# Moving four operand splits of a down projection ahead of the last instructions of the up projection in two engine queues

## The chip, the core and the metric

The kernel runs on one core of one Trainium2 chip. Its engines work side by side, each through a queue of its own in order: TensorE (matrix products, PE in the profile), VectorE (DVE), ScalarE (ACT), GpSimd (POOL) and SyncE (SP), which issues most of the DMA transfers. An instruction that waits holds up everything queued behind it on its engine. The metric is the time of one execution on the device, in microseconds (us); lower is better.

## What is computed

One layer of an encoder for 2304 positions (2048 of one request, 256 of another): a mixer (mLSTM heads and attention heads), and then the feed-forward part, which is where the change lies:

```python
    h = rmsnorm(x, norm2_w)
    u = centred_dwconv(h @ w_up, conv_w, conv_b)
    a, g = jnp.split(u, 2, axis=-1)
    return x + (jax.nn.silu(g) * a) @ w_down
```

`w_up` is 1024 x 5632, `w_down` 2816 x 1024, all in 32-bit floats. The convolution runs over positions with three taps: the centre one and two neighbours.

## The kernel before

**Products in halves.** Each operand of a large product is split in two tiles: a high part, made by a copy to a type with fewer bits on ScalarE, and a low part, the difference of the source and the high part, made on VectorE. A product is then three TensorE instructions: high x high, high x low, low x high. Both operands of a group must be split before its three products are complete. In the down pass this is `halves` (L1395 to L1398): L1397 on ScalarE, L1398 on VectorE.

**Seven products for eight.** The up pass and the down pass each multiply 2 x 2 blocks with seven block products and additions, under the names 11, 21, t2, t1, t3, 22, t4. In the up pass `up_start` (L1204) and its inner `rest` do this for a pair of channel chunks: the products accumulate in three PSUM tiles p1, p2, p3, ScalarE copies them out (`copy`, L1244) and VectorE adds (`add`, L1247). The last three steps of `rest` are the product 22, the add into `u12`, the product t4, and the copy into `u21`. `u12` belongs to the first chunk of the pair, `u21` to the second.

**The up pass** (`phase_u`, L1267) goes over two blocks of positions, and in each over 11 groups of two chunks. A group does `up` for its gate half, a SiLU (L1352), `up` for its other half, and the product of both (L1355). After each `up` comes `conv` (L1323) for both chunks: the centre tap on ScalarE (L1329, which writes `y`), a small copy (L1334), two neighbour taps on VectorE (L1336), and two corrections of one column on ScalarE (L1340) at the border of the two requests. There are three `y` buffers. GpSimd stores the results in tiles `a_d` in DRAM, with four sums and differences of them (L1357 to L1366).

**The down pass** (`phase_e`, L1369) goes over the seven block products, in each over three column groups z, and in each over 11 weight tiles p. For one p it issues 12 products (L1555): four output groups m of three products. Output groups 0 and 1 go to one PSUM tile, 2 and 3 to the next one of four tiles used in turn with the up pass; the second tile is the one that held p1 of the last `up`, which that `up`'s last copy empties. Each p needs one weight tile `we` (raw load `dw`, L1431, four raw buffers; 13 split buffers), and each four p one activation tile `te` (load L1440, four buffers, split in place). `fetch_w(WA)` and `fetch_t(2)` (L1514, L1515) ask for the first two of each ahead of the loop; later ones are asked for within it, the third weight tile during p = 0.

**Memory.** The pools of the down pass lie on the stack where those of the up pass lay: `e_t` (te) from the base, over the operands in `d_1`, then `e_w` (we) and `e_r` (dw). A tile waits only for those older tiles that it overlaps. An operand tile of the up pass takes 18,560 bytes of a partition, a `te` 12,288, a `we` 4,096.

**Order.** The order of instructions on each engine isn't that of the program text. A planner at build time replays the program with modelled durations and lets each engine take the instruction that is ready, the earlier one in the text first. A manual dependency between two instructions of one engine adds no wait on the chip; it only tells the planner which comes first.

Of the kernel before, what the change touches and what calls it, by code (L numbers as in the profile page):

```python
# [11 lines left out]
AF = mybir.ActivationFunctionType  # L12
ALU = mybir.AluOpType
# [22 lines left out]
BLK = 1152  # L36
# [56 lines left out]
def f32(ap):  # L93
    return ap.bitcast(F32)


class Ctx:
    pass


def rstd_of(g, pool, ms, n, name):
# [1038 lines left out]
def n2_ops(pool, b, which):  # L1140

    return {k: pool.tile([P, NCC // 2, 2, NH], F32R, tag="n" + k, name=f"n{k}_{b}", bufs=1) for k in which}
# [61 lines left out]
def up_start(g, s1, bank, ops, b, jj, rs=None):  # L1204


    nc = g.nc
    n = (DT[b + 1] - DT[b]) // 2
    m = n // 2
    nm = f"{b}_{jj}"  # L1210
    r1, r2 = rs or up_load(g, s1, b, jj)
    h = D // 2
    a11, a12, a21, a22 = r1[:, 0:h], r1[:, h:D], r2[:, 0:h], r2[:, h:D]
    t1, t2, t4 = (s1[0].tile([P, h], F32, tag="tmp", name=f"tw{k}_{nm}", bufs=3) for k in (1, 2, 4))

    def mul(p, k, src, add=False):

        i = g.nwu = (g.nwu + 1) % WU
        w = s1[i // 3].tile([P, 2, NCC // 2, P], F32R, tag="wu", name=f"wu{k}_{nm}", bufs=3 if i < 3 else WU - 3)
        hi, lo = (w[:, a].rearrange("p c n -> p (c n)") for a in range(2))  # L1220
        nc.scalar.activation(hi, src, AF.Copy)
        nc.vector.tensor_tensor(lo, src, f32(hi), ALU.subtract)
        for z in range(2):
            for c in range(NCC // 2):
                for i, (aa, bb) in enumerate(((0, 0), (0, 1), (1, 0))):
                    nc.tensor.matmul(p[:, z], w[:, aa, c, :], ops[k][:, c, bb, z * m:z * m + m],  # L1226
                                     start=c == 0 and i == 0 and not add, stop=c == NCC // 2 - 1 and i == 2,
                                     skip_group_check=add)
    p1, p2 = bank("a" + nm)[:, :, 0:m], bank("b" + nm)[:, :, 0:m]
    mul(p1, "11", a11)  # L1230
    mul(p2, "21", a12)

    nc.gpsimd.tensor_tensor(t1, a21, a22, ALU.add)
    nc.gpsimd.tensor_tensor(t2, t1, a11, ALU.subtract)
    nc.gpsimd.tensor_tensor(a21, a11, a21, ALU.subtract)
    nc.gpsimd.tensor_tensor(t4, a12, t2, ALU.subtract)

    def rest(u1, u2):


        u11, u12, u21, u22 = (u[:, k * n:k * n + n].rearrange("p (z t) -> p z t", z=2) for u in (u1, u2) for k in range(2))

        def copy(o, p):
            nc.scalar.activation(o, p, AF.Copy)  # L1244

        def add(o, p, q):
            nc.vector.tensor_tensor(o, p, q, ALU.add)  # L1247
        copy(u11, p1)
        add(u11, p2, u11)
        mul(p1, "t2", t2, True)  # L1250
        copy(u12, p1)
        p3 = bank("c" + nm)[:, :, 0:m]
        mul(p3, "t1", t1)
        copy(u21, p3)
        mul(p1, "t3", a21, True)
        add(u22, p1, u21)
        mul(p3, "22", t4, True)
        add(u12, p3, u12)
        mul(p1, "t4", a22, True)
        copy(u21, p1)  # L1260
    return rest


# [3 lines left out]
def phase_u(g, tc, s1, pd, ops, first):  # L1267


    nc = g.nc  # L1270
    ND = T // BLK
    groups = [list(range(j, j + 2)) for j in range(0, NFC, 2)]
    with ExitStack() as st:
# [14 lines left out]
        cw = cp.tile([P, 4, 2 * NFC], F32, name="cw")  # L1288
        NC = NW - BLK
        carry = cp.tile([P, 2 * NFC, NC], F32, name="carry")  # L1290
        sl = st.enter_context(tc.tile_pool(name="d_l", bufs=1, reuse_waits="tile"))
        late = n2_ops(sl, 0, ("t4", "22"))
        su = st.enter_context(tc.tile_pool(name="d_u", bufs=1, reuse_waits="tile"))
        for k in range(UB):
# [11 lines left out]
        for b in range(ND):  # L1306
            nn = DT[b + 1] - DT[b]
            if b:
                ops = n2_ops(s1[0], b, EARLY)
                ops.update(n2_ops(sl, b, ("t4", "22")))  # L1310
                ops.update(n2_ops(sl2, b, ("t3", "t1")))
                for k, e in zip(OPS, P1):
                    n2_load(g, ops, b, k, engs=e)

            def up(j):

                rest = first.pop(0) if first else up_start(g, s1, bank, ops, b, j)
                us = [su.tile([P, NW], F32, tag="u", name=f"u{b}_{j + k}", bufs=UB) for k in range(2)]
                o = NC if b else 1
                rest(*(u[:, o:o + nn] for u in us))  # L1320
                return [conv(j + k, u) for k, u in enumerate(us)]

            def conv(jj, u):  # L1323
                if b:
                    nc.scalar.activation(u[:, 0:NC], carry[:, jj, :], AF.Copy)
                if b < ND - 1:
                    nc.scalar.activation(carry[:, jj, :], u[:, BLK:NW], AF.Copy)
                y = sa.tile([P, BLK], F32, tag="y", name=f"y{b}_{jj}", bufs=YB)
                nc.scalar.activation(y, u[:, 1:1 + BLK], AF.Identity, scale=cw[:, 1, jj:jj + 1], bias=cw[:, 3, jj:jj + 1])  # L1329
                cut = T1 - b * BLK  # L1330
                if cut < BLK:

                    yc = sp.tile([P, 2], F32, tag="yc", name=f"yc{b}_{jj}", bufs=2)
                    nc.scalar.activation(yc, y[:, cut - 1:cut + 1], AF.Copy)  # L1334
                for k, (s, e) in ((0, (0 if b else 1, BLK)), (2, (0, BLK if b < ND - 1 else BLK - 1))):
                    nc.vector.scalar_tensor_tensor(y[:, s:e], u[:, s + k:e + k], cw[:, k, jj:jj + 1], y[:, s:e],  # L1336
                                                   ALU.mult, ALU.add)
                if cut < BLK:
                    for t, k in ((cut - 1, 0), (cut, 2)):
                        nc.scalar.activation(y[:, t:t + 1], u[:, t + k:t + k + 1], AF.Identity,  # L1340
                                             scale=cw[:, k, jj:jj + 1], bias=yc[:, t - cut + 1:t - cut + 2])
                return y

            def store(k, gi, t):
                nc.gpsimd.dma_start(g.a_d[gi // TG][DOPS.index(k), :, gi % TG, b * HB:(b + 1) * HB], t)

            for gi, gr in enumerate(groups):
                if b < ND - 1 and SG <= gi < SG + NCC // 2:
                    n2_sums(g, sa, b + 1, gi - SG)
                ygs = up(gr[0] + NFC)  # L1350
                for y in ygs:
                    nc.scalar.activation(y, y, AF.Silu)  # L1352
                yas = up(gr[0])
                for y, yg in zip(yas, ygs):
                    nc.vector.tensor_tensor(y, y, yg, ALU.mult)  # L1355
                b11, b12, b21, b22 = (y[:, k * HB:(k + 1) * HB] for y in yas for k in range(2))
                t1, t2, t4 = (sa.tile([P, NH], F32, tag="tc", name=f"tc{k}_{b}_{gi}", bufs=3)[:, 0:HB] for k in (1, 2, 4))  # L1357
                store("11", gi, b11)
                nc.gpsimd.tensor_tensor(t1, b12, b11, ALU.subtract)
                nc.gpsimd.tensor_tensor(t2, b22, t1, ALU.subtract)  # L1360
                for k, t in (("t2", t2), ("21", b21), ("t1", t1)):
                    store(k, gi, t)
                nc.gpsimd.tensor_tensor(b12, b22, b12, ALU.subtract)
                nc.gpsimd.tensor_tensor(t4, b21, t2, ALU.subtract)
                for k, t in (("t3", b12), ("22", b22), ("t4", t4)):
                    store(k, gi, t)  # L1366


def phase_e(g, tc, pd):  # L1369


    nc = g.nc
    h = D // 2
    G3 = TW // CG
    with ExitStack() as st:
# [16 lines left out]
            sy.tile([P, 4], F32, tag="rcol", name=f"place_rcol{k}", bufs=2)  # L1392
        swb = st.enter_context(tc.tile_pool(name="e_v", bufs=1, reuse_waits="tile"))

        def halves(t, src):  # L1395
            lo, hi = t[:, 1], t[:, 0]
            nc.scalar.activation(hi, src, AF.Copy)  # L1397
            nc.vector.tensor_tensor(lo, src, f32(hi), ALU.subtract)  # L1398

        def down(f, o, p):  # L1400
            return g.w_down[0, (2 * p + f) * P:(2 * p + f + 1) * P, o * h:o * h + h]
# [101 lines left out]
        def fetch_w(n):  # L1503
            while wq and n > 0:
                k = wq.pop(0)
                ws[k] = weight(*k)
                n -= 1

        def fetch_t(n):
            while tq and n > 0:  # L1510
                k = tq.pop(0)
                ts[k] = acts(*k)
                n -= 1
        fetch_w(WA)  # L1514
        fetch_t(2)  # L1515
        todo = {}
        SZ = NP * G3

# [11 lines left out]
        for z in range(G3):  # L1530
            e = 2 * SZ + z * NP
            at(e + 3, lambda z=z: resid(0, 0, z))
            at(e + 8, lambda z=z: collect(0, z, squares(0, 0, z)))
            e = 4 * SZ + (z + 1) * NP
# [4 lines left out]
            e = 5 * SZ + (z + 1) * NP  # L1539
            at(e + 2, lambda z=z: resid(1, 1, z))  # L1540
            at(e + 8, lambda z=z: collect(1, z, squares(1, 1, z)))
            e = 6 * SZ + (z + 1) * NP
# [3 lines left out]
        for i, k in enumerate(DOPS):  # L1546
            for z in range(G3):
# [21 lines left out]
                if end:  # L1569
                    fetch_t(1)  # L1570
                    qs = []
                    for m in range(2):
# [5 lines left out]
                        q = squares(0, 1, z, (2 * m, 2 * m + 1))  # L1578
# [224 lines left out]
```

## Time and profile before

| | |
|---|---|
| median of three runs | 3371.0 us (3368.56 to 3371.91) |
| span of the profiled execution, first to last instruction | 3372.4 us |
| TensorE busy in the span | 3271.5 us |
| last product of the up pass ends | 2850.21 us after the span's start |
| first product of the down pass starts | 2857.31 us |
| mean granted TensorE clock over the span | 0.986 |

The page gives a span, and no time of its own, for the profiled execution. A row of a timeline gives start, length (both in us), engine, line, operation, output and inputs, their shapes, the number of instructions, and in brackets how long the engine was idle before it and which instruction ended that. In names, numbers are left out: `te` stands for all activation tiles. L1226 are the products of the up pass, L1555 those of the down pass. A chain of waits goes back from the last instruction to whatever released each step. PEclk is the share of TensorE's clock that was granted; 0.50 means that products take twice as long.

### The profile page before, as it was taken

What the parts mean: (1) busy time and instruction counts of PE and PEld (TensorE: products, weight loads), DVE (VectorE), ACT (ScalarE), POOL (GpSimd) and SP (SyncE); (2) the same over time, 40 slices, a digit from 0 to 9 for tenths busy, and PEclk for the clock granted to TensorE, in tenths of its full rate; (3) what the DMA queues carried; (4) which work ended last, traced back from release to release, by engine and by line L of the source; (5) the groups of instructions that cost most, each with busy time, mean ns of one, the idle gap of its engine ahead of it and who ended that gap; (6) DMA issues with size and microseconds to landing.
All of it is one profiled execution on the core that took longest, in us unless ns stands there. A gap on an engine that the chain in (4) does not pass through costs nothing. (4 is left out here: it accounts for less than half of the span.)

```text
span 3372.4 us, 57131 instructions
## 1 busy us (share of the span) xinstructions
PE 3271.5 (97%) x21366; PEld 3047.6 (90%) x21366; DVE 2403.1 (71%) x3727; ACT 1802.4 (53%) x3781; POOL 1327.6 (39%) x1686
## 2 busy tenths in 40 slices
PE   8899999999999999899999999999999999999998
PEld 6788888888888888788889999999999998999998
DVE  7875687777768788876766778877877776544573
ACT  5545666667666777665552544445555555323331
POOL 8652133213333323211246457645554442851112
PEclk9999999999999999999999999999999999999999
DMA  8765343343336444433347334424322223885563
GB/s 273 229 201 150 94 126 97 105 125 98 113 108 188 130 135 128 123 99 96 103 133 263 129 102 148 127 96 176 107 93 97 100 93 102 302 274 172 164 223 107
DMA packets 300636, 483.03 MB, mean 143 GB/s; under 512 B 36597, under 2 KB 186279, under 8 KB 300359
## 3 DMA queue, kind: packets, MB, share of 16 engines
q1 hardware_dynamic: 247543, 348.34, 32.8%
q0 software_dynamic: 36256, 121.60, 10.8%
q10 hardware_dynamic: 16560, 9.44, 0.9%
q8 instruction: 168, 2.75, 0.3%
q14 instruction: 109, 0.89, 0.1%
HBM read 337.37 MB, written 141.91 MB: 142 GB/s over the span
## 5 line engine op out<-in xcount | busy, mean ns | idle before, releaser
L622 DVE TENSOR_TENSOR pl<-ps,ph 128x512 fp32r<-128x512 f32 x520 | 354.0, 685 | 202.1 <-ACT ps L621 190.3
L1226 PE MATMUL pa<-nt,wut 128*128 128x290 f32 (+1 forms) x3168 | 449.2, 298 | 8.7 <-ACT u L1244 8.6
L620 ACT ACTIVATE ph<-ps 128x512 fp32r<-128x512 f32 x520 | 310.0, 596 | 265.7 <-PE ps L617 253.1
L1226 PEld LDWEIGHTS pa<-nt,wut 128*128 128x128 f32 x3168 | 433.1, 190 | 10.9 <-ACT u L1244 10.6
L591 DVE TENSOR_REDUCE mx<-px 128x1 f32<-128x512 f32 (+1 forms) x528 | 346.5, 674 | 100.0 <-PE px L590 98.0
L1336 DVE SCALAR_TENSOR_TENSOR y<-u,cw,y 128x1152 f32<-128x1152 f32 (+1 forms) x176 | 325.3, 1848 | 39.2 <-ACT yc L1334 17.5
L634 PE MATMUL pv<-ph,v 128*128 128x512 f32 (+1 forms) x1040 | 319.4, 402 | 0.8 <-ACT ph L620 0.3
L621 ACT ACTIVATE ps<-ps 128x512 f32<-128x512 f32 x520 | 310.3, 597 | 0.0
L1555 PE MATMUL et<-tet,wet 128*128 128x384 f32 x1584 | 279.0, 336 | 0.0
L1555 PEld LDWEIGHTS et<-tet,wet 128*128 128x128 f32 x1584 | 277.1, 188 | 0.0
L1069 PEld LDWEIGHTS po<-cmx,wo 128*128 128x128 f32 x1728 | 221.6, 191 | 9.6 <-DVE cmx L1057 1.5
L1069 PE MATMUL po<-cmx,wo 128*128 128x256 f32 x1728 | 225.8, 284 | 1.5 <-DVE cmx L1057 1.3
L1555 PE MATMUL e<-te,we 128*128 128x384 f32 x1188 | 213.9, 341 | 11.0 <-ACT te L1397 7.1
L1555 PEld LDWEIGHTS e<-te,we 128*128 128x128 f32 x1188 | 211.5, 191 | 12.0 <-ACT te L1397 7.3
L616 PE MATMUL ps<-qq,kk 128*128 128x512 f32 x520 | 215.9, 417 | 6.0 <-DVE mx L591 3.8
L780 PE MATMUL mj<-mn,wm 128*128 128x256 f32 x1296 | 200.8, 289 | 9.7 <-DMA mn<-n_d 3.9
L780 PEld LDWEIGHTS mj<-mn,wm 128*128 128x128 f32 x1296 | 185.5, 194 | 26.6 <-issue 6.8
L617 PE MATMUL ps<-qm,kl 65*128 65x512 f32 x520 | 207.6, 401 | 0.0
L590 PE MATMUL px<-kk,qq 128*128 128x512 f32 (+1 forms) x528 | 203.2, 415 | 3.9 <-DVE mx L591 2.6
L790 PEld LDWEIGHTS mv<-wm,mn 128*128 128x128 f32 x1296 | 181.9, 190 | 17.8 <-ACT qb L786 2.3
L790 PE MATMUL mv<-wm,mn 128*128 128x256 f32 x1296 | 194.8, 285 | 0.9 <-ACT qb L786 0.8
L634 PE MATMUL pv<-pl,v 128*128 128x512 f32 x520 | 192.2, 401 | 0.0
(307 smaller groups left out, 7216.9 us busy)
## 6 DMA issues: line engine op xcount, KB each, us to landing
mn<-n_d SPq DMA_DIRECT2D x216, 256.0 KB, 3.4
ru<-w_up SPq DMA_DIRECT2D x88, 512.0 KB, 3.6
a_d<-y POOLq DMA_DIRECT2D x88, 288.0 KB, 2.6
a_d<-tc POOLq DMA_DIRECT2D x66, 288.0 KB, 2.8
n_d<-n1T SPq DMA_DIRECT2D x18, 1024.0 KB, 5.7
dm<-nm_d POOLq DMA_DIRECT2D x72, 256.0 KB, 4.0
mjn<-n_d SPq DMA_DIRECT2D x72, 256.0 KB, 3.5
mvn<-n_d SPq DMA_DIRECT2D x72, 256.0 KB, 3.1
```

Of the source, the lines that this page charges most:

```text
L591: nc.vector.tensor_reduce(s.mx[:, t, z0:z0 + 1], ps[:, 0:w], AX.X, ALU.max)
L616: nc.tensor.matmul(ps, kk[:, kc:kc + P], s.qq[:, 0:N], start=True, stop=False)
L620: nc.scalar.activation(ph, ps, AF.Exp)
L621: nc.scalar.activation(ps, ps, AF.Exp)
L622: nc.vector.tensor_tensor(pl, ps, f32(ph), ALU.subtract)
L634: nc.tensor.matmul(s.pv[0:HD if k in (1, 3) else P, 0:N], v, p, start=(kp == 0 and k == 0), stop=(2 * kp + 2 == s.nk and k == 5))
L780: nc.tensor.matmul(pj[:, o], s.w[c][:, a, o * P:(o + 1) * P], nT[c][:, :, h, :], start=(c + o + k == 0), stop=(c == NCC - 1 and k == 2 and ...
L790: nc.tensor.matmul(pv[:, o], nT[c][:, o, a, :], s.w[c][:, h, 256:512], start=(c + o + k == 0), stop=(c == NCC - 1 and k == 2 and o == 1))
L1069: nc.tensor.matmul(po[:, o], wo[z // 2][c][:, a, n], mx[c][:, h, :], start=(c == 0 and k == 0), stop=(c == NCC - 1 and k == 2))
L1226: nc.tensor.matmul(p[:, z], w[:, aa, c, :], ops[k][:, c, bb, z * m:z * m + m], start=c == 0 and i == 0 and not add, stop=c == NCC // 2 - 1 ...
L1336: nc.vector.scalar_tensor_tensor(y[:, s:e], u[:, s + k:e + k], cw[:, k, jj:jj + 1], y[:, s:e], ALU.mult, ALU.add)
L1555: nc.tensor.matmul(ps[m // 2][:, m % 2], w[:, aa, m * P:(m + 1) * P], t[:, bb], start=p == 0 and n == 0, stop=p == NP - 1 and n == 2)
```

## The change

A helper `queue_behind(tc, later, *earlier)` is added. It gives the instruction `later` a manual dependency, without a wait, on each of `earlier`. The instructions of `rest` and `conv` are now remembered (`g.add12`: the add into `u12`, `g.copy21`: the last copy into `u21`, `g.taps`: centre tap and two neighbour taps of each `conv`; each holds those of the last `up` in the end), and `halves` appends its ScalarE and VectorE instruction to `made`. After the first two weight and activation tiles, three calls are made:

```diff
+def queue_behind(tc, later, *earlier):
+    for e in earlier:
+        tc.add_manual_dep(later.ins, e.ins.name,
+                          mybir.DependencyInfo(mybir.DependencyClass.NoSync, mybir.DependencyReason.DATA), reason="queue")
...
-            add(u12, p3, u12)
+            g.add12 = add(u12, p3, u12)
...
-            copy(u21, p1)
+            g.copy21 = copy(u21, p1)
...
+                g.taps.append(tap)
...
+        made = []
+
         def halves(t, src):
             lo, hi = t[:, 1], t[:, 0]
-            nc.scalar.activation(hi, src, AF.Copy)
-            nc.vector.tensor_tensor(lo, src, f32(hi), ALU.subtract)
+            made.append((nc.scalar.activation(hi, src, AF.Copy), nc.vector.tensor_tensor(lo, src, f32(hi), ALU.subtract)))
...
         fetch_w(WA)
         fetch_t(2)
+        w0, w1, t0, t1 = made
+        queue_behind(tc, g.add12, w0[1], t0[1])
+        queue_behind(tc, g.copy21, w0[0], t0[0], w1[0], t1[0])
+        queue_behind(tc, g.taps[-2][1], w1[1], t1[1])
```

So on VectorE the low parts of the first weight and the first activation tile come ahead of the last `add12`, and those of the second weight and activation tile ahead of the first neighbour tap of the last but one `conv`; on ScalarE all four high parts come ahead of the last copy. Instructions, operands and loads are the same as before.

More of the change, by code (lines that the diff above doesn't have):

```diff
@@ L1243, in copy @@
         def copy(o, p):
-            nc.scalar.activation(o, p, AF.Copy)
+            return nc.scalar.activation(o, p, AF.Copy)
         def add(o, p, q):
-            nc.vector.tensor_tensor(o, p, q, ALU.add)
+            return nc.vector.tensor_tensor(o, p, q, ALU.add)
         copy(u11, p1)
@@ L1291, in phase_u @@
         sl = st.enter_context(tc.tile_pool(name="d_l", bufs=1, reuse_waits="tile"))
+        g.taps = []
         late = n2_ops(sl, 0, ("t4", "22"))
@@ L1328, in conv @@
                 y = sa.tile([P, BLK], F32, tag="y", name=f"y{b}_{jj}", bufs=YB)
-                nc.scalar.activation(y, u[:, 1:1 + BLK], AF.Identity, scale=cw[:, 1, jj:jj + 1], bias=cw[:, 3, jj:jj + 1])
+                tap = [nc.scalar.activation(y, u[:, 1:1 + BLK], AF.Identity, scale=cw[:, 1, jj:jj + 1],
+                                            bias=cw[:, 3, jj:jj + 1])]
                 cut = T1 - b * BLK
@@ L1335, in conv @@
                 for k, (s, e) in ((0, (0 if b else 1, BLK)), (2, (0, BLK if b < ND - 1 else BLK - 1))):
-                    nc.vector.scalar_tensor_tensor(y[:, s:e], u[:, s + k:e + k], cw[:, k, jj:jj + 1], y[:, s:e],
-                                                   ALU.mult, ALU.add)
+                    tap.append(nc.vector.scalar_tensor_tensor(y[:, s:e], u[:, s + k:e + k], cw[:, k, jj:jj + 1], y[:, s:e],
+                                                              ALU.mult, ALU.add))
+                g.taps.append(tap)
                 if cut < BLK:
```

## The prediction

> **What bounds the kernel now.** I read the page's busy shares first, then TensorE's own timeline around the seam between the up pass and the down pass, then the chain of waits over the same stretch, and last the queues of ScalarE, VectorE and SyncE.
>
> ```profile
> PE 3271.5 (97%) x21366; PEld 3047.6 (90%) x21366; DVE 2403.1 (71%) x3727; ACT 1802.4 (53%) x3781; POOL 1327.6 (39%) x1686
> ```
> TensorE is busy 97% of the 3372.4 us, so a local change can only win where TensorE stands still or runs slowly. TensorE's timeline at the seam (start, length, line, count, idle before and what ended it):
>
> ```profile
> 2846.86 3.34 PE L1226 MATMUL pa<-nt,wut 128*128 128x286 f32 x24
> 2857.31 1.01 PE L1555 MATMUL e<-te,we 128*128 128x384 f32 x2 [7.10 <-ACT te L1397]
> 2859.10 24.31 PE L1555 MATMUL e<-te,we 128*128 128x384 f32 x125 [0.79 <-DVE te L1398]
> 2886.48 118.12 PE L1555 MATMUL e<-te,we 128*128 128x384 f32 x665 [3.07 <-DVE we L1398]
> 3004.44 197.76 PE L1555 MATMUL et<-tet,wet 128*128 128x384 f32 x1128
> ```
> The last up product ends at 2850.21. TensorE then waits 7.10 us for the ScalarE half of the first activation split, 0.79 us for its VectorE half, and later 3.07 us for a weight split. From 2886.48 it runs through: what is gained before that point stays gained. The same stretches with the granted clock (length, TensorE busy and count, PEclk, DMA share, GB/s):
>
> ```profile
> 2857.31:2859.10 1.79, 1.00 (x2) 0.50 0.99 346
> 2859.10:2863.93 4.83, 4.83 (x15) 0.50 0.35 138
> 2863.93:2883.41 19.48, 19.48 (x112) 1.00 0.88 312
> 2883.41:2886.48 3.07, 0.00 (x0) 1.00 0.87 313
> 2887.83:2891.24 3.41, 3.41 (x12) 0.50 0.91 291
> ```
> The idle time also costs clock: after each of the two stops some products ran at 0.50. At full clock a product takes 19.48/112 = 0.174 us.
>
> The chain of waits says why TensorE waits 7.10 us:
>
> ```profile
> 2847.06 0.77 DVE u L1247
> 2847.85 1.36 ACT y L1329
> ...
> 2853.14 1.37 DVE y L1355
> ...
> 2854.53 1.35 ACT y L1329
> 2855.88 1.37 ACT te L1397
> ```
> The first activation split is queued on ScalarE behind the centre tap (L1329) of the very last conv. That tap needs a y buffer, which comes free with the product at L1355, and that follows the taps of the conv before. It is queue order, not data. ScalarE's timeline:
>
> ```profile
> 2840.72 0.65 ACT L1244 ACTIVATE u<-pc 128x572 f32<-128x572 f32 x1 [1.73 <-PE pc L1226]
> 2847.85 1.35 ACT L1329 ACTIVATE y<-u,cw 128x1152 f32<-128x1152 f32 x1 [6.48 <-DVE u L1247]
> 2850.24 0.65 ACT L1244 ACTIVATE u<-pa 128x572 f32<-128x572 f32 x1 [0.80 <-PE pa L1226]
> 2850.79 0.62 ACT L1397 ACTIVATE we<-dw 128x512 fp32r<-128x512 f32 x1
> 2853.01 0.61 ACT L1397 ACTIVATE we<-dw 128x512 fp32r<-128x512 f32 x1
> 2855.78 1.47 ACT L1397 ACTIVATE te<-te 128x1536 fp32r<-128x1536 f32 x1
> ```
> ScalarE stands idle for 6.48 us just before, and the data is there. SyncE issued the two weight tiles at 2823.34 and the first activation tile at 2831.17; in the DMA view of 2829 to 2837 (forty columns of 0.2 us) all of it has moved:
>
> ```profile
> 2823.34 0.97 SPq L1431 DMA_DIRECT2D dw<-w_down  x2
> 2831.17 9.25 SPq L1440 DMA_DIRECT2D te<-a_d  x3
> ...
> DMA  0000000000000000063396588999999520000000
> ...
> DMA packets 528, 0.79 MB, mean 98 GB/s; under 512 B 16, under 2 KB 528, under 8 KB 528
> ```
> 0.79 MB is the whole 768 KB tile, and the last busy column ends at 2835.6. The same view of 2838.3 to 2843.4:
>
> ```profile
> DMA packets 633, 0.96 MB, mean 189 GB/s; under 512 B 16, under 2 KB 632, under 8 KB 632
> ...
> te<-a_d SPq DMA_DIRECT2D x1, 576.0 KB, 8.2
> dw<-w_down SPq DMA_DIRECT2D x2, 256.0 KB, 7.4
> ```
> 0.96 MB is more than the second 768 KB tile, which was issued first of these; I take it as landed near 2843. At the latest it came with the third tile (SyncE's timeline from 2838.9):
>
> ```profile
> 2838.97 1.45 SPq L1440 DMA_DIRECT2D te<-a_d  x1
> ```
> 2838.97 + 8.2 = 2847.2.
>
> **The change, part by part.** Nothing is added or removed: four ScalarE copies and four VectorE subtractions change their place. VectorE's timeline gives the other prices and the places that are passed:
>
> ```profile
> 2843.96 0.76 DVE L1247 TENSOR_TENSOR u<-pa,u 128x572 f32<-128x572 f32 x1 [7.58 <-PE pa L1226]
> 2847.06 0.75 DVE L1247 TENSOR_TENSOR u<-pc,u 128x572 f32<-128x572 f32 x1 [2.35 <-PE pc L1226]
> 2849.47 2.87 DVE L1336 SCALAR_TENSOR_TENSOR y<-u,cw,y 128x1152 f32<-128x1152 f32 x2 [1.66 <-ACT yc L1334]
> 2852.26 0.68 DVE L1398 TENSOR_TENSOR we<-dw,we 128x512 fp32r<-128x512 f32 x1
> 2857.29 1.76 DVE L1398 TENSOR_TENSOR te<-te 128x1536 fp32r<-128x1536 f32 x1 [2.19 <-ACT te L1397]
> ...
> 2860.29 3.02 DVE L1398 TENSOR_TENSOR te<-te 128x1536 fp32r<-128x1536 f32 x2
> 2863.23 0.69 DVE L1398 TENSOR_TENSOR we<-dw,we 128x512 fp32r<-128x512 f32 x1
> ```
>
> *ScalarE, 2 x 0.62 + 2 x 1.47 = 4.2 us moved ahead of the last copy.* They start after the copy of 2840.72 (done 2841.4) and lie in the 6.48 us of idle time: both weights by 2842.6, first tile by 2844.1, second by 2845.6 (2848.7 with the late landing). The copy of 2850.24 is not delayed. Cost 0. The buffers lie over the up pass's memory: four activation buffers of 12 KB end inside the third of its three 18.1 KB operands, so the first weight tile and the first two activation tiles wait for no product after the third of the last up group, done by 2838.3 when SyncE issues its second activation tile.
>
> *VectorE, 0.68 + 1.76 us ahead of the last add.* After the add of 2843.96 ends at 2844.7: first weight by 2845.4, a second weight perhaps by 2846.1, first tile by 2847.9. The last add slides from 2847.06 to 2847.9 at most, 0.8 us, and with it the centre tap of 2847.85. TensorE doesn't need either. Cost 0 on the path.
>
> *VectorE, second weight and second tile ahead of the first tap.* 1.76 us from 2848.6: taps from about 2850.4 in place of 2849.47. If the centre tap ends up behind the copy of 2850.24 on ScalarE, they start at 2852.5, 3 us late. Behind them queue the product at L1355, the last conv, and every later split.
>
> *SyncE* issues nothing new, but the fifth and sixth weight loads wait for raw buffers that the two weight splits free; these issues move ahead with them (for the first from 2852.94, where its split ends now, to 2845.4). That helps; I count 0.
>
> *TensorE, first.* All four operands of the first two tiles are ready at 2850.21. Gone: 7.10 + 0.79 idle, and the slow clock: 17 products took 2863.93 - 2857.31 - 0.79 = 5.83 us and take 17 x 0.174 = 2.96 at full clock, so 2.87. Together **-10.8 us**.
>
> *TensorE, next late.* A weight tile feeds 12 products, 2.09 us. The third is wanted at 2850.21 + 4.18 = 2854.4. Its raw data is there (2840.46 + 7.4 = 2847.9), its split is not moved. On VectorE it comes behind the taps (2.87): with taps from 2850.4 they end at 2853.2, the third activation tile's 1.76 may go first, then 0.68: ready 2855.7, a stop of 1.3. With taps from 2852.5: 2856.0, or 2857.8 behind that tile, or 2859.1 behind L1355's 1.37 as well: a stop of 4.7. A stop can cost clock too: after 2886.48, 12 products took 3.41 instead of 2.09, 1.3 us. Ends: 0 and 6.0. I take **+2.3**, between the stops of 1.3 and 3.4 that have the third tile ahead, since VectorE's timeline puts that tile (the second of the two at 2860.29) directly ahead of the third weight at 2863.23; whether the centre tap comes early or late it can't tell.
>
> *The stop of 3.07 us* hangs on the eleventh weight tile. SyncE's queue:
>
> ```profile
> 2869.92 0.52 SPq L1440 DMA_DIRECT2D te<-a_d  x1
> 2870.62 2.38 SPq L1431 DMA_DIRECT2D dw<-w_down  x3
> ```
> Its load is the first of those three. It stands behind the fifth activation load, which waits until TensorE has done four weight tiles with the first activation buffer; so it moves with TensorE, and I take **0**. The stop can vanish together with its 1.3 us of slow clock (-4.4), since VectorE has 2 x 0.68 + 2 x 1.76 = 4.9 us less to do behind the seam; it can grow by the 3 us that late taps carry on.
>
> [...]
>
> Sum: -10.8 + 2.3 + 0 = -8.5 us. The span of the profiled execution, 3372.4, lies 1.4 above the median of 3371.0; what lies around the span isn't shown. I set the sum against the median: **3362.5 us**. A measurement of this kernel tells about 0.2% (6.7 us) from no change.
>
> **The rivals.**
>
> *A. TensorE starves sooner.* The late order of taps, third tile and L1355, with slow clock: 6.0 given back at the third weight tile, the rest equal: -4.8, 3366.2 us. For it: in the order of before the taps, L1355 and the third tile all stand ahead of the third weight's split. Against: its raw data lies ready from 2847.9 and ScalarE is free after 2850.9.
>
> *B. The second stop goes too*, because the weight stream runs ahead: -8.5 - 4.4 = -12.9, 3358.1 us. For it: the earlier raw buffers, VectorE's 4.9 us. Against: the eleventh load waits for TensorE's own progress.
>
> *C. It doesn't do what it says.* The order says that the splits come ahead of the copy, not what else comes ahead of them. If a later weight's split is put in front, whose buffer the last up product holds until 2850.21, the first tile follows then: ScalarE 0.65 + 0.62 + 1.47, VectorE 1.76: complete at 2854.7, against 2859.05. It wins 4.4 us less the third tile's wait, about -2: 3369 us.
>
> *D. Slower: the copy of 2850.24 becomes the wait.* It empties the PSUM bank that the products of the second half of the columns write, after 6 products (1.0 us). It now stands behind the second activation tile. This decides nothing while that tile lands before 2850.21 - 1.47 = 2848.7; the traced 2843 to 2847.2 leaves 1.5 us at least. To lose 6.7 us against before, the seventh product, due at 2851.3, would have to come 6.7 + 10.8 us late; the tile would land near 2866, 19 us after its latest bound. From that point on it is slower: 3378 us.
>
> **How the numbers follow.** Forecast 0.48; A 0.27; B 0.13; C 0.07; D 0.05. Faster by over 0.2% are the forecast and B: 0.61. Within: A and C: 0.34. Slower: 0.05. The range goes from B's neighbourhood (3357.5) to just short of C (3368.5); the forecast's own is 3360 to 3364.
>
> **What would show it.** The first split of te before 2846 on ScalarE, its VectorE half before 2849; no idle time before the first e product, the clock at 1.00 through 2850 to 2854; the last add up to 0.8 us late; a stop of 1 to 5 us about the third weight tile; a later stop like the 3.07 us one, some 8 us earlier; TensorE unbroken after it. The forecast is wrong if the first split still stands behind the last conv's centre tap, if TensorE stands at its seventh product for the copy, or if the stop at the third weight exceeds 6 us.

## The result, and the profile after

The changed kernel takes 3363.97 us (median of 15 runs, 3356.9 to 3371.05), the kernel before, run beside it, 3370.59 (15 runs): ratio 0.9983, 95% interval 0.9976 to 0.9991. That is 6.6 us less; 3362.5 was forecast.

The page after (busy time of each engine) and TensorE's timeline at the seam:

```profile
PE 3265.5 (97%) x21366; PEld 3043.9 (91%) x21366; DVE 2400.8 (71%) x3727; ACT 1800.9 (54%) x3781; POOL 1327.2 (39%) x1686
```

```profile
2840.19 3.34 PE L1232 MATMUL pa<-nt,wut 128*128 128x286 f32 x24
2843.37 46.33 PE L1569 MATMUL e<-te,we 128*128 128x384 f32 x264
2900.01 94.46 PE L1569 MATMUL e<-te,we 128*128 128x384 f32 x528 [10.31 <-ACT c L1577]
```

The stops of 7.10, 0.79 and 3.07 us are gone: 264 products, which are two whole column groups, run without a break. Then TensorE stands 10.31 us, longer than at any of them. The instruction that ends the stop, `c` at L1577, is the copy of a finished column group out of PSUM, in `update`. The same stretch in windows (length, busy time of PE, PEld, DVE, ACT, POOL with counts, granted clock, DMA share, GB/s):

```profile
2843.37:2889.70 46.33, 46.33 (x266) 46.00 (x264) 27.77 (x24) 19.94 (x27) 21.62 (x24) 1.00 0.73 236
2889.70:2893.86 4.16, 0.00 (x0) 0.00 (x0) 3.06 (x1) 0.00 (x0) 4.13 (x6) 1.00 0.81 244
2893.86:2900.01 6.15, 0.00 (x0) 0.00 (x1) 0.72 (x1) 2.23 (x3) 5.14 (x8) 0.50 0.68 266
2900.01:2904.10 4.09, 4.09 (x13) 4.09 (x14) 1.04 (x1) 2.05 (x3) 2.66 (x6) 0.50 0.49 167
```

The clock is granted in full up to the stop, falls to 0.50 within it, and the first 4.09 us of running after it go at half speed, which loses 2.0.

**Where the copies stand.** ScalarE's timeline of the changed kernel, and SyncE's row of the activation loads:

```profile
2888.20 1.17 ACT L1408 ACTIVATE te<-te 128x1152 fp32r<-128x1152 f32 x1 [2.80 <-DMA te<-a_d]
2897.78 1.48 ACT L1408 ACTIVATE te<-te 128x1536 fp32r<-128x1536 f32 x1 [8.41 <-DMA te<-a_d]
2899.17 2.90 ACT L1577 ACTIVATE c<-e 128x768 f32<-128x768 f32 x4
```

```profile
2866.64 23.60 SPq L1450 DMA_DIRECT2D te<-a_d  x4
```

The four copies (of column groups 0 and 1 of the first block product) stand behind the high part of an activation tile, the first of the second block product. Its load is the last of those four issues, at about 2889.7: its buffer comes free only when TensorE ends column group 1. TensorE cannot begin group 2, whose PSUM banks are those of group 0, before the copies; the copies wait for a split; the split waits for a load that TensorE's own progress releases. From its end of work to its next product pass a load of 8 us, a split and a copy. In the kernel before, the first two copies stand two tiles sooner in the queue, behind a split that waited for its load too:

```profile
2903.32 1.49 ACT L1397 ACTIVATE te<-te 128x1536 fp32r<-128x1536 f32 x1 [3.25 <-DMA te<-a_d]
2904.71 1.49 ACT L1563 ACTIVATE c<-e 128x768 f32<-128x768 f32 x2
```

But TensorE reached group 2 only at about 2912 (137 products after 2886.48), some 6 us after these copies.

**The second thing that moved** is the tail of the up pass. VectorE and ScalarE of the changed kernel:

```profile
2845.31 1.36 DVE L1408 TENSOR_TENSOR te<-te 128x1152 fp32r<-128x1152 f32 x1 [2.07 <-ACT te L1408]
2847.06 1.90 DVE L1408 TENSOR_TENSOR we<-dw,we 128x512 fp32r<-128x512 f32 x3 [0.40 <-ACT we L1408]
2848.88 1.41 DVE L1344 SCALAR_TENSOR_TENSOR y<-u,cw,y 128x1152 f32<-128x1152 f32 x1
2850.20 1.75 DVE L1408 TENSOR_TENSOR te<-te 128x1536 fp32r<-128x1536 f32 x1
...
2852.48 1.41 DVE L1344 SCALAR_TENSOR_TENSOR y<-u,cw,y 128x1151 f32<-128x1151 f32 x1
...
2855.61 1.35 DVE L1364 TENSOR_TENSOR y<-y,y 128x1152 f32<-128x1152 f32 x1
```

```profile
2843.57 0.65 ACT L1250 ACTIVATE u<-pa 128x572 f32<-128x572 f32 x1 [5.08 <-PE pa L1232]
2844.11 1.16 ACT L1408 ACTIVATE te<-te 128x1152 fp32r<-128x1152 f32 x1
2845.17 1.35 ACT L1336 ACTIVATE y<-u,cw 128x1152 f32<-128x1152 f32 x1
...
2859.13 1.49 ACT L1408 ACTIVATE te<-te 128x1536 fp32r<-128x1536 f32 x1 [3.28 <-DMA te<-a_d]
2860.52 1.34 ACT L1336 ACTIVATE y<-u,cw 128x1152 f32<-128x1152 f32 x1
...
2868.51 1.17 ACT L1408 ACTIVATE te<-te 128x1152 fp32r<-128x1152 f32 x1 [5.00 <-DMA te<-a_d]
2869.59 0.65 ACT L1349 ACTIVATE y<-u,yc,cw 128x1 f32<-128x1 f32 x2
```

The planner let splits that nobody had moved go first: the third activation tile and weights three to five ahead of the neighbour taps, the fourth activation tile between them, the fifth ahead of the last centre tap, the sixth ahead of the last corrections of one column. The splits of the fifth and the sixth wait for loads. So the stores slide. GpSimd, first before, then after:

```profile
2866.30 4.26 POOL L1409 DMA_DIRECT2D ds<-w_down  x8 [8.67 <-ACT y L1340]
...
2886.38 0.54 POOL L1345 DMA_DIRECT2D a_d<-tc  x1
```

```profile
2870.53 4.26 POOL L1419 DMA_DIRECT2D ds<-w_down  x8 [10.40 <-ACT y L1349]
...
2889.70 0.54 POOL L1354 DMA_DIRECT2D a_d<-tc  x1
```

Counted from the end of the up products (2850.21 before, 2843.53 after), the last store is issued at +46.2 us in place of +36.2, and GpSimd's weight loads at +27.0 in place of +16.1. In the memory plan the target of the first copies lies over the up pass's `y` and `tc` buffers, so the copies must wait for that store too (e2 below shows this wait).

**How the runs are compared.** The instructions up to the seam have the same order in both kernels, yet the up products end at 2850.2 and 2850.5 in two profiles of before and between 2837.7 and 2846.5 in the twelve others. On average before ends them 7.4 us later, and 5.2 of these are granted clock: ahead of the seam, running at a clock of 0.50 cost TensorE 30.5 and 30.4 us in the two profiles of before and 18.7 to 29.9 in the twelve others. Without this loss TensorE was busy there for 2739.6 to 2742.0 us in all fourteen. Why the clock fell more or less often no run shows. The medians hardly show such a gain: over the twelve runs the median falls by 1.4 us more on average than the time behind the seam (against the mean of the two profiles of before). All profiles are counted from the end of the up products.

### The profile page after: what moved, and what is told of

Same layout as the page of the kernel before. It is cut to its first block, busy times and chain, and to the rows that moved or that the text cites. A ratio compares the mean times of both kernels' runs of the same rounds, so it can differ in the third digit from the quotient of the medians.

```text
span 3362.6 us, 57130 instructions
## 1 busy us (share of the span) xinstructions
PE 3265.5 (97%) x21366; PEld 3043.9 (91%) x21366; DVE 2400.8 (71%) x3727; ACT 1800.9 (54%) x3781; POOL 1327.2 (39%) x1686
## 5 line engine op out<-in xcount | busy, mean ns | idle before, releaser
L1569 PE MATMUL e<-te,we 128*128 128x384 f32 x1188 | 211.3, 338 | 10.3 <-ACT c L1577 10.3
```

The costliest lines, as they stand in the source:

```text
L1569: nc.tensor.matmul(ps[m // 2][:, m % 2], w[:, aa, m * P:(m + 1) * P], t[:, bb], start=p == 0 and n == 0, stop=p == NP - 1 and n == 2)
```

## The experiments

Theory Q: the copies' place in ScalarE's queue makes the new stop. Theory M: the late stores make it, through the memory under the copies' target.

The ratio is to the kernel before, run beside each (its medians lay between 3368.0 and 3370.6 us). "To the end" is the time from the last up product to the end of the span; "stops" are TensorE's idle times over 0.4 us in the 300 us after that product; "half speed" is half of the time that it ran at a clock of 0.50 there; "rest" is what remains.

| kernel | median us | ratio, 95% interval | to the end | stops | half speed | rest |
|---|---|---|---|---|---|---|
| before, first profile | | | 522.2 | 11.0 | 4.6 | 506.6 |
| before_again | 3369.1 | 0.9996 (0.9988 to 1.0005) | 524.3 | 11.9 | 4.2 | 508.3 |
| after | 3364.0 | 0.9983 (0.9976 to 0.9991) | 519.1 | 10.3 | 2.0 | 506.7 |
| after_again | 3362.2 | 0.9983 (0.9973 to 0.9993) | 518.7 | 8.1 | 2.9 | 507.7 |
| e1_memory | 3365.1 | 0.9988 (0.9979 to 0.9997) | 516.3 | 7.4 | 1.7 | 507.2 |
| e2_copy_first | 3353.7 | 0.9954 (0.9942 to 0.9966) | 514.3 | 3.6 | 1.7 | 509.0 |
| e12_tail_only | 3364.4 | 0.9984 (0.9976 to 0.9993) | 518.7 | 7.9 | 2.6 | 508.1 |
| e7_tail_copy | 3355.3 | 0.9952 (0.9939 to 0.9964) | 508.9 | 0.7 | 0 | 508.2 |
| e4_first_pair | 3364.1 | 0.9984 (0.9972 to 0.9996) | 519.5 | 7.9 | 2.5 | 509.1 |
| e5_memory_copy | 3362.5 | 0.9977 (0.9968 to 0.9986) | 517.9 | 7.7 | 2.4 | 507.8 |
| e6_memory_copy_early | 3360.3 | 0.9973 (0.9962 to 0.9985) | 515.2 | 5.0 | 2.3 | 507.9 |
| e10_no_sums | 3364.4 | 0.9985 (0.9975 to 0.9994) | 518.2 | 7.8 | 2.0 | 508.5 |
| e9_taps_copy | 3357.4 | 0.9969 (0.9958 to 0.9981) | 514.6 | 4.4 | 1.7 | 508.5 |
| e11_taps_weight | 3361.3 | 0.9977 (0.9968 to 0.9986) | 518.2 | 6.7 | 3.3 | 508.2 |

The last column is the key to all that follows: it is 506.6 to 509.1 in all fourteen profiles. What a kernel gains or loses behind the seam is its stops and the slow clock around them, within some 2 us.

**The two kernels again.**

> The kernel before, profiled a second time. All readings so far compare one profile of it with several of the changed kernel. If the stops at the seam belong to the kernel and not to the run, it shows again about 7 us of TensorE idle ahead of the first down product, then stops of about 0.8 and 3 us, and 520 to 524 us from the end of the up products to the end of the span (522.19 in the first profile). If the second profile lies at 517 or lower there, the difference of 3 us between the first two profiles is no measure of the change.

> The changed kernel once more, for a second profile and more times. Both theories expect the stop ahead of the third column group of the down pass again: about 10 us with some 2 us lost to slow clock behind it, and 8 to 12 us of idle time less at the seam than before the change. From the end of the last up product to the end of the span 518 to 520 us, as in the first profile (2843.53 to 3362.6, 519.1). If the 10.3 us stop was an accident of that one execution, this run shows under 2 us there and a span some 12 us shorter behind the seam.

TensorE's timeline of before, second profile:

```profile
2857.57 1.01 PE L1555 MATMUL e<-te,we 128*128 128x384 f32 x2 [7.10 <-ACT te L1397]
...
2887.61 118.00 PE L1555 MATMUL e<-te,we 128*128 128x384 f32 x665 [3.50 <-DVE we L1398]
```

Both sets of stops come back in the second profiles, so they belong to the kernels. Before loses 15.6 and 16.0 us at the seam, after 12.4 and 11.0.

**Only the memory (e1).** The block that is written first gets another place:

```diff
-        quad = {k: sc.tile([P, 4, TW], F32, name="c%d%d" % k) for k in ((0, 1), (0, 0), (1, 0), (1, 1))}
+        quad = {k: sc.tile([P, 4, TW], F32, name="c%d%d" % k) for k in ((0, 0), (1, 0), (1, 1), (0, 1))}
```

> Only the place of four accumulator tiles in memory is changed: the one that the first copies out of PSUM fill no longer lies over the up pass's y and tc buffers, but over an operand that the last up product frees. Theory Q (queue): the copies of the first column group stand on ScalarE behind the high part of an activation tile whose load starts only when TensorE has finished the second column group; the order on ScalarE is unchanged here, so the stop stays at 10.3 us (9 to 11.5) and the time is that of the changed kernel within 0.1%. Theory M (memory): the copies wait for the last stores out of the y and tc buffers; the stop goes (under 2 us) and the time falls by 10 to 12 us.

A stop of 7.40 us stays, ended by the same copy, directly behind the same split (2897.81 on ScalarE, the copy at 2899.20). The stores are not what ends the stop. It is shorter than the 9 us that Q asked for at least, but after_again, with the memory of the change, shows 8.13.

**Only the place of the copies (e2).**

```diff
+        queue_behind(tc, te_hi[1, 0, 0], c0[0, 0, 0], c0[0, 0, 1])
```

Here `te_hi` and `c0` are the split and the copies, remembered where they are made.

> Only the order on ScalarE is changed: the copies of the first column group come ahead of the high part of the first activation tile of the next block product. Theory Q: the copies no longer wait for that load; what is left is the landing of the last store out of the tc buffers, issued when the second column group ends, about 4 us: stop 4 to 6 us, time 4 to 7 us under the changed kernel's. Theory M: the stores alone set the copies, so the stop stays at 9 to 11 us and the time is unchanged.

TensorE, then ScalarE:

```profile
2887.47 72.84 PE L1570 MATMUL e<-te,we 128*128 128x384 f32 x406 [3.61 <-ACT c L1578]
```

```profile
2883.09 1.17 ACT L1408 ACTIVATE te<-te 128x1152 fp32r<-128x1152 f32 x1 [2.33 <-DMA te<-a_d]
2886.61 2.92 ACT L1578 ACTIVATE c<-e 128x768 f32<-128x768 f32 x4 [2.35 <-DMA a_d<-tc]
2889.39 1.50 ACT L1408 ACTIVATE te<-te 128x1536 fp32r<-128x1536 f32 x1
```

One call of `queue_behind` that adds no work takes the stop to 3.61 us. What ends the copies' wait is now a store out of `tc`: M is the second wait, hidden behind Q until then.

**Tail early, with the copies behind the split (e12) and ahead of it (e7).** Both queue the fifth activation tile's high part behind the last columns' correction:

```diff
+        queue_behind(tc, te_hi[0, 1, 1], g.fix)
```

In e12 then follows

```diff
+        for z, m in ((0, 0), (0, 1), (1, 0), (1, 1)):
+            queue_behind(tc, c0[0, z, m], te_hi[1, 0, 0])
```

and in e7

```diff
+        queue_behind(tc, te_hi[1, 0, 0], c0[0, 0, 0], c0[0, 0, 1])
```

> The tail of the up pass comes early, as in the kernel before with both edits, but the copies of the first two column groups stay behind the split whose load waits for TensorE, as in the change. Theory Q: the place on ScalarE alone makes the stop, so 7 to 9 us of it stay at +53 to +57 us, ended by the copy, though the stores have landed some 10 us before. Theory M alone (the stores make the stop): it shrinks to under 2 us. The whole from the end of the up products to the end of the span: 515 to 519 us by Q, 508 to 511 by M.

> The copies of the first two column groups go ahead of the split that they stood behind, as in the best run so far, and the high part of the fifth activation tile goes behind the last convolution's edge columns, so that the up pass's last stores are issued earlier; the memory plan is that of the change. Theory M as second wait (copies wait for the last store out of the up pass's buffers, which landed 2.9 us before the copies ended the stop): with the stores some 5 us earlier the stop of 3.61 us shrinks to at most 1 us, and 510 to 513 us pass from the end of the up products to the end of the span. If the edge columns were not what the stores wait for, the stop stays at 3 to 4 us and the time is that of the best run.

TensorE in e12, ScalarE in e12, TensorE in e7:

```profile
2899.30 60.87 PE L1570 MATMUL e<-te,we 128*128 128x384 f32 x333 [7.90 <-ACT c L1578]
```

```profile
2890.01 1.17 ACT L1408 ACTIVATE te<-te 128x1152 fp32r<-128x1152 f32 x1 [4.90 <-DMA te<-a_d]
2897.07 1.48 ACT L1408 ACTIVATE te<-te 128x1536 fp32r<-128x1536 f32 x1 [5.89 <-DMA te<-a_d]
```

```profile
2844.57 46.33 PE L1570 MATMUL e<-te,we 128*128 128x384 f32 x264
2891.63 68.64 PE L1570 MATMUL e<-te,we 128*128 128x384 f32 x391 [0.73 <-ACT c L1578]
```

With the after profiles these are the four corners. In e12 the last store leaves at +41.2 and lands at +46.1 us, and the copies still start only at +53.2, behind the split: the early tail alone gains nothing (518.7 against 519.1 and 518.7). Early copies alone gain 4 to 5 us; both together 10. In e7 every stop but 0.73 us is gone. It is 14 us faster than the kernel before, against 7 to 8 for the change alone, and the intervals of the two ratios do not meet. e2, with 16, can't be told from it by the medians (their intervals overlap); behind the seam e7 is 5.4 us shorter. Both profiles are of the median run, and ahead of the seam, where the two kernels are alike, the clock of 0.50 cost e2 19.5 us and e7 28.0: in these two runs it is that, and not the seam, that brings e2 level.

**Only the first pair of splits moved (e4).** The calls keep `w0` and `t0` and drop `w1` and `t1`.

> Only the first weight tile and the first activation tile are put ahead; the second pair is left where the planner puts it. Theory Q (the stop at the third column group comes from copies out of PSUM that stand on ScalarE behind a split whose load waits for TensorE): the order of the copies is the one of the changed kernel, so the stop of 7 to 10 us stays, and the time is that of the changed kernel within 2 us. A rival to my reading of the gain: the second pair is needed for the stop of 0.79 us and the one of 3.07 us to go; then these two come back (about 4 us more than the changed kernel).

Time and new stop (7.34 us, ended by the copy) are those of the change. The first weight and the first activation tile are enough for the gain, and for the harm. The planner put the second weight tile's split ahead all the same (ScalarE does both weights from 2830.46), so what e4 moves back is the second activation tile alone.

**Early copies and other memory, without the early tail (e5, e6).** e5 is e1 and e2 together; e6 puts the copies ahead of two more splits.

> Both: the accumulator's other place in memory and the copies ahead of that activation split. Theory Q: no store and no load is left to wait for; the stop is under 1.5 us, no slow clock behind it, 11 to 13 us under the changed kernel's time, 14 to 18 us under the time before. Theory M: the same as with the memory change alone. If the stop has a third cause, it is still over 4 us here.

> The copies of the first two column groups are queued ahead of the last two activation tiles of the first block as well (in the run before they still stood behind the split of the last of them, which waited for its load), and their target is memory that is free early. Theory Q with M: the copies start as soon as the column group ends, so no stop between +40 and +60 us after the up products, where the run before had 2.44 us. Theory D (VectorE's low parts take two to seven times as long where GpSimd adds weights next to them, and this moves with every shift): a stop of 3 to 6 us can still come at +90 to +105 us. Q and M alone: 510 to 514 us from the end of the up products to the end of the span; with D's stop again 515 to 518.

e5 missed: 2.44 us stayed where the copies now stood behind one more late split, and 5.28 us of new stops came 50 us later. e6 took the first away, not the second. TensorE in e6:

```profile
2843.69 92.48 PE L1570 MATMUL e<-te,we 128*128 128x384 f32 x528
2939.40 0.69 PE L1570 MATMUL e<-te,we 128*128 128x384 f32 x1 [3.22 <-ACT te L1408]
2941.19 19.08 PE L1570 MATMUL e<-te,we 128*128 128x384 f32 x98 [1.10 <-DVE te L1408]
```

Its groups of VectorE's low parts from 2904 to 2947 (line, engine, operation, shapes, count, then busy us and mean ns) show parts that take twice as long as the 1.76 and 0.69 us of other places, with GpSimd's sums beside them:

```profile
L1408 DVE TENSOR_TENSOR te<-te 128x1536 fp32r<-128x1536 f32 x3 | 10.9, 3628 | 22.7 <-ACT te L1408 22.7
L1408 DVE TENSOR_TENSOR we<-dw,we 128x512 fp32r<-128x512 f32 x5 | 7.3, 1500 | 2.2 <-ACT we L1408 2.2
```

**Is it the sums (e10)?** e6 with the four `nc.gpsimd.tensor_tensor` of `sums` taken out.

> The run with early copies and freed memory, in which TensorE stood 4.3 us at +95 to +98 us, without GpSimd's four sums for each weight row (its loads and stores stay, so the later products get plain weights in place of summed ones). Theory D (the stop comes from VectorE's low parts, which take up to three times as long beside GpSimd's sums, and what is queued behind them): the low parts stay at 1.76 us for 128x1536 and 0.69 us for 128x512, and the stop at +95 goes or falls under 1 us, 510 to 513 us from the end of the up products to the end of the span. Theory L (the stop comes from loads: the late tail puts GpSimd's weight loads next to the activation tiles' loads): the low parts are fast, and the stop stays at 3 us or more.

The same groups, 2902 to 2945, and TensorE:

```profile
L1408 DVE TENSOR_TENSOR we<-dw,we 128x512 fp32r<-128x512 f32 x9 | 5.9, 687 | 5.6 <-ACT we L1408 5.6
L1408 DVE TENSOR_TENSOR te<-te 128x1536 fp32r<-128x1536 f32 x3 | 5.3, 1758 | 27.2 <-ACT te L1408 27.2
```

```profile
2941.71 0.69 PE L1566 MATMUL e<-te,we 128*128 128x384 f32 x1 [4.57 <-ACT te L1408]
```

The sums do stretch the low parts: 3628 and 1500 ns with them, 1758 and 687 without. But the stop is longer than in e6 (4.57 and 1.10 us, with two more of 1.35 and 0.76 ahead of it). In both kernels its larger part is ended by the tile's high part, on ScalarE, which waits for a load: D falls as the cause of that part. By its trace D stays a part of the cause in e5: there 4.00 of the 5.28 us are ended by the tile's low part, which took 4.41 us beside the sums. In e6 and e10, with low parts of 1.76 us, that wait is 1.10. What goes with the late stop is the load of the activation tile that TensorE wants there (issues in the DMA view: kilobytes of each, us to landing), in e7 and in e10:

```profile
te<-a_d SPq DMA_DIRECT2D x1, 768.0 KB, 9.2
```

```profile
te<-a_d SPq DMA_DIRECT2D x1, 768.0 KB, 14.7
```

It was issued at +77.2 us in e7, +78.9 in e2, +81.7 in e6, +81.9 in e5, +83.7 in e10, and took 9.2, 10.1, 12.3, 12.8 and 14.7 us; the first two have no late stop, the others have. In e7 one group of four of GpSimd's weight loads (1 MB) starts between +75 and +87 us, in the other four kernels two. That fits L, and e2 says that two groups alone do not make a stop. No run moved these loads by themselves, so how much is start and how much company stays open.

**Taps first (e9, e11).** e9 is e7 with the third activation tile behind the first convolution's taps; e11 is the change with that tile and the third weight tile behind them:

```diff
+        for hi, lo in made[4:6]:
+            queue_behind(tc, hi, g.taps[-2][0])
+            queue_behind(tc, lo, *g.taps[-2][1:])
```

> As the best two runs together with the third activation tile behind the first convolution's taps, but the third weight tile left ahead of them: the taps come some 2 us earlier, TensorE wants the third activation tile only at +16.6 us. Expected: a stop under 1 us at the third weight, none at +46 to +57 us, and 507 to 510 us from the end of the up products to the end of the span, 13 to 16 us faster than the kernel before. If the copies of the first column groups still wait for the last store, a stop of 0.7 to 3 us at +47 us.

> The change, with the third activation tile and the third weight tile queued behind the first convolution's taps: the order on which my forecast was made. The working of that step gives, with the copy of the last sum at +0.7 us, the taps at +6.4 and +8.4 and the third weight's low part at +10.4 where TensorE wants it at +4.0: a stop of 5.5 to 7 us there, slow clock after it, and then no further stop, since the last stores come early again and the copies stand ahead of the split. 511 to 515 us from the end of the up products to the end of the span. If the early tail isn't what keeps the later stop away, the stop of 7 to 10 us at +54 us comes as well, and the time is that of the kernel before or more.

e9 missed: 0.85 us at +47, but a late stop of 0.54 and 3.04 us; the load above was issued at +78.1 and took 14.2 us, with two groups of GpSimd's loads beside it, and the 3.04 us are ended by a low part that took 3.44 us beside the sums. TensorE in e11:

```profile
2850.80 0.62 PE L1569 MATMUL e<-te,we 128*128 128x384 f32 x2 [1.20 <-ACT te L1408]
2854.66 42.80 PE L1569 MATMUL e<-te,we 128*128 128x384 f32 x234 [3.25 <-DVE we L1408]
2899.74 60.44 PE L1569 MATMUL e<-te,we 128*128 128x384 f32 x336 [2.27 <-ACT c L1577]
```

This order costs 4.45 us about the third weight tile (the second of the two stops is ended by its low part), 1 less than I expected. The stop of the copies shrinks to 2.27 us and does not vanish: they wait there for the split of the first block's last tile. From the end of the up products to the end of the span 511 to 515 us were expected and 518.2 came.

## Why the prediction was right, and where it was not

The time lay 1.5 us from the forecast, and only part of the reasons held. The ratio is a fall of 0.17%, just short of the 0.2% from which the prediction counts a kernel as faster (0.61, against 0.34 for a smaller change); its interval lies clear of 1.

- *TensorE, first* (-10.8): right. The first down product follows the last up product at once, at full clock. Before loses 7.10 + 0.79 us and the slow clock there in both profiles; no kernel with the change does. e4 adds that the second activation tile need not come ahead for it.
- *TensorE, next late* (+2.3, between 0 and 6.0): wrong, 0. The step took the taps to come ahead of the third activation tile and the third weight tile. The planner put both splits ahead of the taps, and the third weight's low part was ready as it was wanted. With the third tile and the third weight put behind the taps by hand (e11) the stops are 4.45 us and the clock of 0.50 takes 1.7 more: 6.2, by the upper end of my range and not the 2.3 that I took. So the order was wrong, and the price too low.
- *The stop of 3.07 us* (0, with -4.4 as the other end): wrong, it went, in all kernels with the change. It is the term of rival B, which was given 0.13. VectorE in before, just ahead of the stop's end at 2886.48:

```profile
2876.85 3.69 DVE L1398 TENSOR_TENSOR we<-dw,we 128x512 fp32r<-128x512 f32 x1 [5.06 <-ACT we L1397]
2880.77 3.99 DVE L1398 TENSOR_TENSOR te<-te 128x1536 fp32r<-128x1536 f32 x1 [0.23 <-ACT te L1397]
```

Such low parts took 0.69 and 1.76 us at 2863.23 and 2857.29, and GpSimd's sums run beside these from 2872.93. In the changed kernel TensorE is through the first column group, which needs the eleventh weight, by about 2866.5, and GpSimd's first sum starts at 2880.09. That the slow low parts made the stop fits this, but no run tests it by itself.

- *VectorE, no cost on the path*: wrong, and this is the largest error. I named what queues behind the late taps (the product, the last convolution, every later split) and followed it no further than the third weight. The stores came 10 us later against the seam, and the order on ScalarE changed 55 us on: a copy that freed PSUM landed behind a split that waited for TensorE. That is 10.31 us of stop and 2.0 of slow clock, in no rival. Rival D had the same shape (a copy out of PSUM behind an activation split that waits for its load), at the wrong place; D's own copy cost 0.56 us in e4 and nothing in the change.
- *Sum*: the stop of 3.07 us was worth 4.8 and not 4.4, since half of the 3.41 us at a clock of 0.50 is 1.7 (the twelve products that I counted there include some cut by the window's edges). So by the profiles -10.8 - 4.8 + 10.3 + 2.0 = -3.3; from the seam to the end 522.19 became 519.10, -3.1. The second pair of profiles gives 524.31 to 518.74, -5.6. The medians give -6.6 and -7.8; what they fall by beyond the seam is not explained. I forecast -8.5 with two errors of opposite sign, a second stop that went and a new one that I did not see, and with a part of the medians' fall, 1 to 5 us, that is in no term. That the number came out is luck.

## What to carry to other kernels

Where a planner orders the queues, a dependency on two instructions moves others too: after such a change compare the whole order on each engine, and look for an instruction that frees a buffer and stands behind one that waits for the very engine that needs the buffer. The cure was one more call of the same kind (e2) or two (e7). Behind the seam they were worth 4 to 5 and 10 us, the change itself 3 to 6. Sum up a bottleneck engine's stops and slow clock first: if the rest is constant over the variants (here 506.6 to 509.1 us), the list of stops and slow clock is the whole account. Look which instruction ends each stop before naming one cause for all: the late stops here were ended by a high part in e6 and e10 and mostly by a stretched low part in e5 and e9.

## What the runs showed of the hardware

- Stops behind the seam and a clock of 0.50. In the first profile of before the clock of 0.50 lasted 10.24 us about the stop of 7.10 us, from 3.49 us into it, and 3.41 us after the stop of 3.07 us, from 1.35 us after its end. In the first profile of the changed kernel it lasted 10.24 us about the stop of 10.31 us, from 4.16 us into it. What it cost did not grow with the stop ("half speed" in the table): 1.7 us with one of 3.61 us (e2) and one of 7.40 (e1), 2.6 with 7.90 (e12), 2.0 with 10.31 (after), and none with 0.73 (e7). Behind the stop of 2.44 us in e5, 264 products took 46.45 us, against 46.33 ahead of it; behind the one of 2.27 us in e11, 336 took 60.44 us, by my estimate from the same 46.33 us some 1.5 more than at full clock.
- A low part of 128x1536 on VectorE took 1.76 us in before (at 2857.29), and 3.63 on average in a stretch of e6 where GpSimd's sums run; without the sums the same stretch showed 1.758 (e10).
- A load of 768 KB took 9.2 (e7) to 14.7 us (e10) from issue to landing in the same place of six kernels that differ in the order of their queues (three also in one place in memory, one of these in the sums).
